# Six stages of a two-layer diffusion trunk in a new order: opening, short convolutions, attention's end, first head, output projections' banks, last token tile

## The chip, the cores and the metric

The kernel runs on one core of one Trainium2 chip. The time is the device time of one execution in microseconds, lower is better; what is compared is the median of several executions of the same program. The core has five engines with queues of their own: TensorE (PE, matrix products into PSUM), VectorE (DVE), ScalarE (ACT), GpSimd (POOL) and SyncE (SP), whose queue issues almost all of this kernel's transfers.

## The reference

Two groups of tokens, 128 prompt tokens and 1024 latent tokens of 1024 features, go through the same two layers in float32. The modulation of each layer (six vectors per group: shift, scale, gate for the mixer and for the feed-forward part) is a product of a condition vector with w_mod.

```python
for l in range(DEPTH):                      # DEPTH = 2
    sh1, sc1, gt1, sh2, sc2, gt2 = split(silu(cond) @ w_mod[l] + b_mod[l], 6)
    h = x * (1 + sc1) + sh1
    if l % 2 == 0:
        q, k, v, bg, cg, xi = split(h @ w_in)       # 8 heads, 2 KV heads, width 64
        att = attend(rope(rms(q)), rope(rms(k)), v) # latent tokens also see 256 cached keys
        o = concat([att, bg * dwconv(cg * xi)]) @ w_out
    else:
        o = hgrn(h)                                 # two directions of a gated recurrence
    x = layer_norm(ALPHA * x + gt1 * o)
    a, g = split(dwconv((x * (1 + sc2) + sh2) @ w_up))
    x = layer_norm(ALPHA * x + gt2 * ((silu(g) * a) @ w_down))
```

dwconv is a convolution over three neighbouring tokens, feature by feature. The outputs are x of both groups, the prompt's keys and values and the recurrence's states.

## The kernel before

**Tiling.** The nine token tiles of 128 (tile 0 the prompt, 1 to 8 the latent tokens) are kept as transposed activations with features on the partitions; a product for one block of 128 output features runs over three chunks of some 386 token columns (c = 0, 1, 2) and eight blocks of the contraction (k). Every product of the large matrices is made of three matmuls on split operands, hi x hi, hi x lo and lo x hi (`mm3`, L92 to L95). A weight block is loaded by `wraw` (L97: 512 KB, two buffers, SP's queue) and split by `wsplit` (L103): the rounded part hi by ACT (L108), the remainder lo by POOL or DVE (L109).

**Opening** (L369 to L516). Per block b of the contraction the first modulation is computed (`modulation`, L415), the activations are modulated and transposed (`modulate`, L444), and the key columns' products of that block are put between (psk, 3 banks). The pool pdS has 5 banks. The value columns (j = 5) follow after the opening in full (`feature`, L516).

**Query, keys, values and short convolutions** (L527 to L671). For each of four groups of 128 features three features are computed (L648 on): the first is copied by ACT, the second multiplied by it (pr, L658) and convolved by ACT and two DVE taps (L661, L662), the third multiplied by the result (sc, L667). Beside them stand seven chunks of later modulation. A chunk (`mod_chunk`, L146) is four loads of 512 KB into two buffers, 16 accumulations on DVE (macc, L170 and L172), eight transposes on TensorE (L181), two reductions (L183) and two additions (L184). `mod_steps` (L190) does the same for the feed-forward layers with loads of 256 KB and eight matmuls against a column of ones (L220).

**Attention** (L673 to L897). Steps of scores, exponentials (ACT), probability tiles PT and value products; PE and ACT issue in written order there (`manual_schedule`, L861). Inside such a region the named engines issue in the order of the program; for all others, and outside, a planner orders the instructions by simulated costs. Every fifth PT is copied by ACT and rounded by POOL (L797 on). Behind the steps a group's finish (L823 to L859) transposes the outputs, scales them and stores them, split, as rows of rhsa. The convolution sums are split into rhsb (L889 to L895: ACT for hi, POOL and DVE in turn for lo).

**Output projection** (`out_projection`, L919). Eight units of weights (two blocks of k and half the columns each); units 0 and 1 are loaded in here, unit n > 2 in a ring of five. The first half of the columns is computed for tiles 8, 7, 6 ahead of the rest. `pt_` (2 banks, transpositions) is opened before `pd` (3 pairs of banks, psd).

**Feed-forward** (`ffn_up`, L1011, and `ffn_down`, L1310). ffn_up has N0 = 6 plain features and then products with combined operands; the first four operands (`operand`, L1110: hi by ACT L1126, lo by POOL) are made behind conv(4). In ffn_down the last token tile is handled like the others: `settle`, L1461 (gate), `ln_sums` (L262), then `ln_affine` (L307).

**Recurrence** (L1527 on). In the first head five jobs of the layer norm are put between chunk steps (list later0, L1889). `recurrence_out` (L2041) has the same two pools as out_projection; jobs in its list todo are taken at t < 2 in addition. `tail1` (L2099) is the last layer norm's affine step.

## Time and profile before

| what | us |
|---|---|
| median of 3 executions | 3229.24 (3228.61 to 3229.68) |
| the profiled execution, its own time | 3231.56 |
| its span, first to last instruction | 3229.8 |
| TensorE busy in it | 3131.4 (97%) |
| DVE, POOL, ACT busy | 2264.6, 1414.8, 1284.4 |
| mean granted clock of TensorE | 0.99 |

TensorE bounds nearly all of the span, so the views to read are those that show where it does not run or runs at the lower clock: its waits by releaser, and the table of stretches, which has the granted clock beside the busy time. Only then are the timelines of the other engines of use, each at one of those places, to see what the engine that released TensorE had done until then. The tail behind the last matmul is read from the timelines of DVE, ACT and POOL.

### The profile page before, as it was taken

To read this page: it belongs to the slowest core of one execution; us is meant where nothing else is said; L and a number is where in the kernel's file an instruction comes from. 1 tells how busy PE (TensorE), PEld (TensorE's weight loads), DVE (VectorE), ACT (ScalarE), POOL (GpSimd) and SP (SyncE) were. 2 spreads that over 40 slices of the span, in tenths; PEclk is the share of its full clock that TensorE was granted. 3 is DMA by queue.
4 is the path that set the end of the run, shared out by engine and by line. 5 is a ranking of instruction groups with operands and counts; after the bars stand their busy time and mean duration, and the time that the engine had idled before them with its cause. 6 is when DMAs were issued, how large, how long until landed. Compare 5 with 4: busy or idle time off the path is not lost. (4 is left out here: it accounts for less than half of the span.)

```text
span 3229.8 us, 48748 instructions
## 1 busy us (share of the span) xinstructions
PE 3131.4 (97%) x19231; PEld 2909.9 (90%) x19231; DVE 2264.6 (70%) x3111; ACT 1284.4 (40%) x2165; POOL 1414.8 (44%) x1014
## 2 busy tenths in 40 slices
PE   7999999899999999999999999999999999999997
PEld 6998788789999998887999999999779999998886
DVE  6777888538988875676566676655656889675356
ACT  4410988333333334215433334333544333335112
POOL 6721233335545443573244343333425554444464
PEclk9999999999999999999999999999999999999999
DMA  7143000322322326542222222211331323225452
GB/s 218 41 132 97 1 1 1 124 85 65 95 89 93 87 97 207 179 160 71 97 83 80 65 68 79 63 51 44 125 118 48 96 84 98 67 78 191 151 172 80
DMA packets 267477, 305.42 MB, mean 95 GB/s; under 512 B 19588, under 2 KB 200016, under 8 KB 267249
## 3 DMA queue, kind: packets, MB, share of 16 engines
q1 hardware_dynamic: 266160, 299.49, 29.2%
q8 instruction: 152, 2.49, 0.3%
q0 software_dynamic: 1088, 2.82, 0.3%
q14 instruction: 77, 0.62, 0.1%
...
## 5 line engine op out<-in xcount | busy, mean ns | idle before, releaser
L1127 POOL TENSOR_TENSOR wlo<-S,whi 128x512 fp32r<-128x512 f32 x152 | 243.1, 1613 | 252.5 <-ACT whi L1126 251.8
L109 POOL TENSOR_TENSOR wlo<-wraw,whi 128x1024 fp32r<-128x1024 f32 x78 | 197.3, 2533 | 206.2 <-ACT whi L108 206.1
L93 PE MATMUL psd<-whi,s 128*128 128x512 f32 x720 | 283.8, 394 | 1.0 <-DVE u L1271 0.9
L95 PE MATMUL psd<-whi,s 128*128 128x512 f32 x720 | 283.8, 394 | 0.0
L94 PE MATMUL psd<-wlo,s 128*128 128x512 f32 x720 | 283.8, 394 | 0.0
L1155 DVE SCALAR_TENSOR_TENSOR t<-u,fcw,t 128x1156 f32<-128x1156 f32 x152 | 264.8, 1760 | 13.8 <-ACT t L1150 11.1
L95 PE MATMUL psq<-T,wlo 128*128 128x290 f32 x912 | 270.7, 297 | 0.0
L94 PE MATMUL psq<-T,whi 128*128 128x290 f32 x912 | 270.2, 296 | 0.0
L93 PE MATMUL psq<-T,whi 128*128 128x290 f32 x912 | 270.0, 296 | 0.0
L1682 POOL TENSOR_TENSOR X<-X,tot 128x384 f32<-128x384 f32 x144 | 169.3, 1176 | 225.3 <-PE pss L1676 212.4
L1127 POOL TENSOR_TENSOR wlo<-wraw,whi 128x512 fp32r<-128x512 f32 x114 | 183.1, 1606 | 171.6 <-ACT whi L1126 153.7
L108 ACT ACTIVATE whi<-wraw 128x1024 fp32r<-128x1024 f32 x130 | 136.8, 1054 | 289.6 <-DMA wraw<-in_ffn_w_down_dram 118.8
L1126 ACT ACTIVATE whi<-S 128x512 fp32r<-128x512 f32 x152 | 92.9, 627 | 321.4 <-DVE S L1105 247.2
L1385 DVE TENSOR_TENSOR y<-y,psd 128x512 f32<-128x512 f32 x144 | 97.9, 684 | 168.0 <-PE psd L95 167.4
L213 DVE SCALAR_TENSOR_TENSOR macc<-mraw,sil,macc 128x512 f32<-128x512 f32 x182 | 189.5, 1080 | 9.0 <-DMA mraw<-in_w_mod_dram 9.0
L93 PE MATMUL psu<-h,whi 128*128 128x388 f32 (+1 forms) x504 | 176.6, 351 | 11.6 <-DVE sc L667 6.5
L94 PE MATMUL psu<-h,whi 128*128 128x388 f32 (+1 forms) x504 | 176.0, 349 | 2.0 <-POOL h L456 2.0
L93 PE MATMUL psp<-s,whi 128*128 128x384 f32 x480 | 174.7, 364 | 0.0
L95 PE MATMUL psu<-h,wlo 128*128 128x388 f32 (+1 forms) x504 | 174.6, 346 | 0.0
L1682 DVE TENSOR_TENSOR X<-X,tot 128x384 f32<-128x384 f32 x144 | 111.6, 775 | 88.0 <-PE pss L1676 85.8
L94 PEld LDWEIGHTS psq<-T,whi 128*128 128x128 f32 x912 | 172.2, 189 | 0.0
L93 PE MATMUL psp<-h,whi 128*128 128x384 f32 x480 | 172.2, 359 | 0.0
...
## 6 DMA issues: line engine op xcount, KB each, us to landing
...
```

Of the source, the lines that this page charges most:

```text
L93: mm(ps, l[0], r[0], start=start, stop=False)
L94: mm(ps, l[0], r[1], start=False, stop=False)
L95: mm(ps, l[1], r[0], start=False, stop=stop)
L108: nc.scalar.activation(hi[:, :n], raw[:, :n], AF.Copy)
L109: (eng or nc.gpsimd).tensor_tensor(lo[:, :n], raw[:, :n], r32(hi[:, :n]), op=ALU.subtract)
L213: nc.vector.scalar_tensor_tensor(acc[:, cond, :], raw, sil[:, cond, k:k + 1], acc[:, cond, :], op0=ALU.mult, op1=ALU.add)
L1126: nc.scalar.activation(hi, src, AF.Copy)
L1127: nc.gpsimd.tensor_tensor(lo, src, r32(hi), op=ALU.subtract)
L1155: nc.vector.scalar_tensor_tensor(t, u[:, :, c0:c0 + HO], taps(p + NF * x)[c0], t, op0=ALU.mult, op1=ALU.add)
L1385: nc.vector.tensor_tensor(y[t][:, cols], y[t][:, cols], ps, op=ALU.add)
L1682: eng.tensor_tensor(x, x, t4[:, :, :, 1 - half].unsqueeze(3).to_broadcast([P, 2, nb, hh]), op=ALU.mult)
```

## The change

Six places are rewritten; what is computed stays the same.

- Opening: the value columns of chunks c = 2 and 1 are accumulated beside the keys in a pool of their own (puV, psv, 2 banks; pdS shrinks from 5 to 3), c = 0 follows after it; their sums are copied by ACT first thing in the next stage.
- Short convolutions: the seven chunks are made by `mod_steps`, whose last step (the matmuls and the addition) is put off by one place (`ends`); the region has a written order for DVE and PE, with 7 to 18 steps per group.
- Attention's end: the last five PT tiles do not go by POOL; the last steps, the first two weight units of the output projection, the finish and the splitting of the convolution sums (DVE alone) are in written order on all engines.
- First head: the place at which the jobs of later0 are taken moves.
- Output projections: the pools pd and pt_ change places; the first products of out_projection run by halves of k; one extra job of recurrence_out is taken at t = 4 instead of t = 0; in ffn_up operand 0 precedes conv(4).
- Last token tile of layer 1: sums, statistics and affine step by halves of the columns, in PSUM.

```diff
...
-    def mod_steps(chunks, pool, bank, bufs=1, steps=1):
+    def mod_steps(chunks, pool, bank, bufs=1, steps=1, ends=None):
...
                 if k == 0:
-                    acc = pool.tile([P, 2, 512], F32, tag="macc", name="macc")
+                    acc = pool.tile([P, 2, 512], F32, tag="macc", bufs=1 if ends is None else 2, name="macc")
...
                 load()
+            def end(l=l, c0=c0, acc=acc):
+                ps = bank()
+                for cond in range(2):
+                    for f in range(4):
+                        mm(ps[:, 4 * cond + f:4 * cond + f + 1], acc[:, cond, f * P:(f + 1) * P], ones, start=True,
+                           stop=True)
+                nc.vector.tensor_tensor(mods[:, l, :, c0:c0 + 4], ps[:, 0:8].rearrange("p (c f) -> p c f", f=4),
+                                        colA[:, l * 48 + c0:l * 48 + c0 + 4].unsqueeze(1).to_broadcast([P, 2, 4]),
+                                        op=ALU.add)
+            if ends is not None:
+                ends.append(end)
+                continue
             yield from [True] * steps
...
+            end()
...
+    qv = ExitStack()
+    pv = qv.enter_context(tc.tile_pool(name="puV", reuse_waits="tile", bufs=1, space=PSUM))
     with ExitStack() as st:
-        pd = st.enter_context(tc.tile_pool(name="pdS", reuse_waits="tile", bufs=5, space=PSUM))
+        pd = st.enter_context(tc.tile_pool(name="pdS", reuse_waits="tile", bufs=3, space=PSUM))
...
         psk = pu.tile([P, 3, 512], F32, tag="u", name="psu")
+        psv = pv.tile([P, 2, 512], F32, tag="v", name="psv")
...
                     b == 0, b == KT - 1)
+            for c in (2, 1):
+                a = 1 + c * OW
+                mm3(psv[:, c - 1, :OW], (wval[0][:, b, :], wval[1][:, b, :]), (hT[0].k(b, a, OW), hT[1].k(b, a, OW)),
+                    b == 0, b == KT - 1)
...
         wkey = wload(wcols(w_in, 512), KT, P)
+        wval = wload(wcols(w_in, 640), KT, P)
...
         st.enter_context(qk)
+        fTv = wk.tile([P, SW], F32, tag="fT", bufs=2, name="fT")
+        nc.scalar.activation(fTv[:, OW:].rearrange("p (a b) -> p a b", b=OW), psv[:, :, :OW], AF.Copy)
+        qv.close()
...
         for j in (4, 5, 0, 1, 2, 3):
-            ps = psk if j == 4 else feature(pus[(j + 1) % 2], j * P, OW, 1)
-            fT = work([P, SW], "fT")
-            nc.scalar.activation(fT.rearrange("p (a b) -> p a b", b=OW), ps[:, :, :OW], AF.Copy)
+            if j == 5:
+                ps, fT = pus[0].tile([P, 3, 512], F32, tag="u", name="psu"), fTv
+                for k in range(KT):
+                    mm3(ps[:, 0, :OW], (wval[0][:, k, :], wval[1][:, k, :]),
+                        (hT[0].k(k, 1, OW), hT[1].k(k, 1, OW)), k == 0, k == KT - 1)
+                nc.scalar.activation(fT[:, :OW], ps[:, 0, :OW], AF.Copy)
+            else:
+                ps = psk if j == 4 else feature(pus[(j + 1) % 2], j * P, OW, 1)
+                fT = work([P, SW], "fT")
+                nc.scalar.activation(fT.rearrange("p (a b) -> p a b", b=OW), ps[:, :, :OW], AF.Copy)
...
+    oun = []
+    def out_unit(n):
+        hf, kk = n // 4, n % 4
+        return (ins["attn_w_out"][0][2 * kk * P:2 * (kk + 1) * P, hf * 512:(hf + 1) * 512]
+                .rearrange("(k p) f -> p k f", p=P), 2, 512)
...
         wk = st.enter_context(tc.tile_pool(name="wkc", reuse_waits="tile", bufs=1))
-        accp, mbufs = wk, 2
...
         pd = st.enter_context(tc.tile_pool(name="pdC0", reuse_waits="tile", bufs=2, space=PSUM))
-        for j in range(4):
+        ends = []
+        mod = mod_steps([mod_todo.pop(0) for _ in range(7)], wk, lambda: pd.tile([P, 512], F32, tag="d", name="mps"), 4,
+                        1, ends)
+        def beside(n):
+            old = list(ends)
+            ends.clear()
+            for _ in range(n):
+                next(mod, None)
+            for f in old:
+                f()
+        st.enter_context(tc.manual_schedule(engines={ET.DVE, ET.PE}))
+        for j, (n0, n1, n2) in enumerate(((1, 3, 3), (6, 6, 6), (6, 6, 6), (7, 7, 0))):
...
             nc.scalar.activation(cg, ps[:, :, :IW], AF.Copy)
-            mod_finish(1)
-            mod_chunk(*mod_todo.pop(0), pd, "d")
+            beside(n0)
...
             nc.vector.scalar_tensor_tensor(yv, pr[:, :, 2:2 + OW], cw[2], yv, op0=ALU.mult, op1=ALU.add)
-            mod_finish(1)
-            if j < 3:
-                mod_chunk(*mod_todo.pop(0), pd, "d")
+            beside(n1)
...
                                     op=ALU.mult)
-        mod_finish()
+            beside(n2)
+        beside(0)
+        assert next(mod, None) is None and not ends
...
             PTs[i] = PT
-            if i % 5 == 5 - 1:
+            if i % 5 == 5 - 1 and i < len(steps) - 5:
...
+        PVL = 4
+        total = len(steps)
+        def step(i):
+            p = i + LEAD
...
+            turn["after"] = piece(*pieces[p]) if 0 <= p < total else None
         with tc.manual_schedule(engines={ET.PE, ET.Activation}):
...
-        for i in sorted(later):
-            for f in later[i]:
-                f()
+            for i in range(-LEAD - 3, total - 1):
+                step(i)
         rhsb = [hp.tile([P, 4, PW], F32R, tag=f"h{q}1", name=f"rb{q}") for q in range(2)]
-        for a, b in ((768, SW), (384, 768), (0, 384)):
+        def second(a, b):
...
                 nc.scalar.activation(hi, sc32[:, j, a:b], AF.Copy)
-                (nc.vector if j % 2 else nc.gpsimd).tensor_tensor(rhsb[1][:, j, a:b], sc32[:, j, a:b], r32(hi),
-                                                                  op=ALU.subtract)
+                nc.vector.tensor_tensor(rhsb[1][:, j, a:b], sc32[:, j, a:b], r32(hi), op=ALU.subtract)
+        with tc.manual_schedule(engines=ALL):
+            raws = [wraw(*out_unit(n)) for n in range(2)]
+            step(total - 1)
+            step(total)
+            oun.append(wsplit(*raws[0], eng=nc.vector))
+            for i in range(total + 1, total + PVL):
+                step(i)
+            oun.append(wsplit(*raws[1], eng=nc.vector))
+            ends = [f for i in sorted(later) for f in later[i]]
+            for f in ends[:2]:
+                f()
+            second(768, SW)
+            for f in ends[2:]:
+                f()
+            for a in (384, 0):
+                second(a, a + 384)
...
         wk = prj.enter_context(tc.tile_pool(name="wk3", reuse_waits="tile", bufs=1))
+        pd = prj.enter_context(tc.tile_pool(name="pdB", reuse_waits="tile", bufs=3, space=PSUM))
         pt_ = prj.enter_context(tc.tile_pool(name="ptB", reuse_waits="tile", bufs=2, space=PSUM))
-        pd = prj.enter_context(tc.tile_pool(name="pdB", reuse_waits="tile", bufs=3, space=PSUM))
...
         def w_unit(n):
-            hf, kk = n // 4, n % 4
-            return wload(w_out[2 * kk * P:2 * (kk + 1) * P, hf * 512:(hf + 1) * 512]
-                         .rearrange("(k p) f -> p k f", p=P), 2, 512, (wk, 5) if n > 2 else None,
-                         nc.vector if n % 2 else None)
+            return wload(*out_unit(n), (wk, 5) if n > 2 else None, nc.vector if n % 2 else None)
...
         rows = wk.tile([P, 2, D], F32, name="rows")
-        units = [w_unit(n) for n in range(2)]
+        units = oun
...
 
-        def products(t, hf):
+        def products(t, hf, ks=range(KT)):
             o = oidx(t)
-            if hf == 0:
+            if t not in pss:
                 pss[t] = pd.tile([P, 2, 512], F32, tag="d", name="psd")
-            for k in range(KT):
+            for k in ks:
...
 
-        for t in (8, 7, 6):
-            products(t, 0)
+        for ks in (range(4), range(4, KT)):
+            for t in (8, 7, 6):
+                products(t, 0, ks)
...
                 nc.sync.dma_start(sd[l][n // 2 - 1], cvs.pop(n - 2))
+            if n == N0 - 1:
+                pr[P0] = (raws.pop(N0 + 1)[0], raws.pop(N0)[0])
+                operand(0)
...
             if n == N0 - 1:
-                pr[P0] = (raws.pop(N0 + 1)[0], raws.pop(N0)[0])
-                for o in range(4):
+                for o in range(1, 4):
...
+            def last_tile():
+                add, st = nc.vector.tensor_tensor, lp.tile([P, 2, 6], F32, tag="bst", name="bst")
+                mv = lp.tile([P, 4], F32, tag="bmw", name="bmw")
+                ps = pw.tile([P, 2, 512], F32, tag="w", name="psw")
+                halves = [slice(hf * 512, (hf + 1) * 512) for hf in range(2)]
+                def sums(hf):
+                    p = ps[:, hf, :]
+                    add(p, p, rows[:, cond_of(0), halves[hf]], op=ALU.mult)
+                    add(p, p, y[0][:, halves[hf]], op=ALU.add)
+                products(ps[:, 0, :], gi, 0, [NU - 4, NU - 3])
+                for f in behind:
+                    f()
+                end[0]()
+                sums(0)
+                end[1]()
+                nc.vector.bn_stats(st[:, 0, :], ps[:, 0, :])
+                products(ps[:, 1, :], gi, 0, [NU - 2, NU - 1])
+                sums(1)
+                nc.vector.bn_stats(st[:, 1, :], ps[:, 1, :])
+                nc.vector.bn_aggr(mv[:, 0:2], st)
+                nc.vector.tensor_scalar(mv[:, 2:3], mv[:, 1:2], EPS, None, op0=ALU.add)
+                x = x1_tile()
+                def one(a, op, cols):
+                    nc.gpsimd.tensor_tensor(x[:, cols], (x if a else y[1])[:, cols], gb[:, a, cols], op=op)
+                one(0, ALU.mult, halves[0])
+                nc.gpsimd.tensor_tensor(mv[:, 3:4], mv[:, 2:3], mhalf[:, 0:1], op=ALU.pow)
+                one(0, ALU.mult, halves[1])
+                for hf, cols in enumerate(halves):
+                    nc.vector.scalar_tensor_tensor(ps[:, hf, :], ps[:, hf, :], mv[:, 0:1], gb[:, 0, cols],
+                                                   op0=ALU.subtract, op1=ALU.mult)
+                for hf, cols in enumerate(halves):
+                    nc.vector.scalar_tensor_tensor(y[0][:, cols], ps[:, hf, :], mv[:, 3:4], gb[:, 1, cols],
+                                                   op0=ALU.mult, op1=ALU.add)
+                    nc.sync.dma_start(outs[0][0][:, cols], y[0][:, cols])
+                for cols in halves:
+                    one(1, ALU.add, cols)
+                    nc.sync.dma_start(outs[1][0, 0:P, cols], x[:, cols])
             for t in range(NT - 1, -1, -1):
+                if l and t == 0:
+                    last_tile()
+                    return y
...
             for n, _ in enumerate(chunk_steps(w0[a], evs[a], c)):
-                if later0 and n % 4 == 1 and (c < 2 or a or n > 4):
+                if later0 and n % 4 == 1 and (c < 2 or 8 * a + n > (4, 12)[len(later0) == 4]):
...
     def recurrence_out():
+        pd = prj.enter_context(tc.tile_pool(name="pdH", reuse_waits="tile", bufs=3, space=PSUM))
         pt_ = prj.enter_context(tc.tile_pool(name="ptH", reuse_waits="tile", bufs=2, space=PSUM))
-        pd = prj.enter_context(tc.tile_pool(name="pdH", reuse_waits="tile", bufs=3, space=PSUM))
...
                     todo.pop(0)(pbank, tmp)
-                if hf and todo and t < 2:
+                if hf and todo and t in (4, 1):
...
         v, g = nc.vector, nc.gpsimd
-        eng = [(slice(0, 512), (v, v)), (slice(512, D), (v, g))] if t == 0 else [(slice(0, D), (v, g))]
-        return [lambda: ln_affine(y[t], gb, x1_tile(), dst, eng)]
+        return [lambda: ln_affine(y[t], gb, x1_tile(), dst, [(slice(0, D), (v, g))])]
...
```

## Rows read from the trace of the kernel before

**Rows 1.** The page's first section: engine, busy us, share of the span, instructions.

```profile
PE 3131.4 (97%) x19231; PEld 2909.9 (90%) x19231; DVE 2264.6 (70%) x3111; ACT 1284.4 (40%) x2165; POOL 1414.8 (44%) x1014
```

**Rows 2.** TensorE's waits, whole span: tile and line, releaser, us, times, longest.

```profile
PE psu L93 <- DVE sc L667: 6.5, 1, 6.5
PE pss L348 <- ACT psw L285: 4.7, 1, 4.7
...
PE psq L93 <- ACT whi L1126: 3.1, 2, 1.6
PE psl L348 <- DVE ht L356: 2.8, 3, 1.6
```

**Rows 3.** Table of stretches: PE, PEld, DVE, ACT, POOL busy, granted clock, DMA, GB/s.

```profile
16.00:56.00 40.00, 33.20 (x191) 24.55 (x192) 27.98 (x43) 22.98 (x38) 22.44 (x20) 0.87 1.10 304
...
224.00:232.00 8.00, 6.02 (x26) 5.70 (x25) 8.00 (x11) 2.21 (x2) 3.17 (x1) 0.79 0.76 194
240.00:256.00 16.00, 9.54 (x42) 9.29 (x41) 12.48 (x19) 2.09 (x2) 2.34 (x1) 0.68 0.65 189
...
576.00:596.00 20.00, 11.54 (x36) 8.07 (x35) 14.67 (x12) 10.40 (x19) 13.07 (x9) 0.66 0.47 157
2408.00:2420.00 12.00, 8.92 (x37) 8.05 (x36) 7.88 (x20) 6.36 (x8) 3.88 (x4) 0.72 0.30 89
```

**Rows 4.** Timeline of TensorE: start, us, line, operation, count; two stretches.

```profile
194.83 0.34 PE L93 MATMUL psu<-h,whi 128*128 128x388 f32 x1
...
196.95 1.04 PE L181 MATMUL mps<-ident,macc 128*128 128x128 f32 x8
...
908.78 1.84 PE L220 MATMUL psq<-ones,macc 128*128 128x1 f32 x16
```

**Rows 5.** Timeline of DVE in the convolutions; in brackets idle before and releaser.

```profile
185.62 3.55 DVE L172 SCALAR_TENSOR_TENSOR macc<-mraw,sil,macc 128x512 f32<-128x512 f32 x2
...
243.01 4.04 DVE L172 SCALAR_TENSOR_TENSOR macc<-mraw,sil,macc 128x512 f32<-128x512 f32 x4 [5.59 <-DMA mraw<-in_w_mod_dram]
246.97 1.35 DVE L667 TENSOR_TENSOR sc<-psu,yv 128x1158 f32<-128x1158 f32 x1
```

**Rows 6.** Groups of DVE's instructions, 143.8 to 318.6 us: busy us, mean ns.

```profile
L172 DVE SCALAR_TENSOR_TENSOR macc<-mraw,sil,macc 128x512 f32<-128x512 f32 x98 | 77.8, 854 | 13.7 <-DMA mraw<-in_w_mod_dram 13.7
L183 DVE TENSOR_REDUCE mods<-mps 128x4 f32<-128x512 f32 x12 | 7.7, 679 | 7.3 <-PE mps L181 7.3
```

**Rows 7.** Timeline of POOL, the same convolution.

```profile
185.32 2.64 POOL L109 TENSOR_TENSOR wlo<-wraw,whi 128x1024 fp32r<-128x1024 f32 x1 [10.32 <-ACT whi L108]
```

**Rows 8.** Timeline of ACT at attention's end.

```profile
575.76 2.60 ACT L893 ACTIVATE rb<-sc 128x390 fp32r<-128x390 f32 x6
...
591.66 1.06 ACT L108 ACTIVATE whi<-wraw 128x1024 fp32r<-128x1024 f32 x1 [2.18 <-DMA wraw<-in_attn_w_out_dram]
...
606.33 1.06 ACT L108 ACTIVATE whi<-wraw 128x1024 fp32r<-128x1024 f32 x1 [5.03 <-DMA wraw<-in_attn_w_out_dram]
```

**Rows 9.** Timeline of DVE at attention's end.

```profile
576.73 3.93 DVE L894 TENSOR_TENSOR rb<-sc,rb 128x390 fp32r<-128x390 f32 x3
...
584.40 3.36 DVE L109 TENSOR_TENSOR wlo<-wraw,whi 128x1024 fp32r<-128x1024 f32 x1
```

**Rows 10.** Timeline of DVE at the first operands of ffn_up, layer 0.

```profile
789.68 4.45 DVE L1071 TENSOR_TENSOR ra<-held,ra 128x580 fp32r<-128x580 f32 x3
```

**Rows 11.** Timeline of DVE at the last token tile.

```profile
3214.72 1.22 DVE L1461 TENSOR_TENSOR psw<-psw,rows 128x1024 f32<-128x1024 f32 x1
...
3221.11 2.78 DVE L311 TENSOR_TENSOR x<-y,gb 128x512 f32<-128x512 f32 x1 [0.23 <-ACT y L293]
```

**Rows 12.** Timeline of POOL at the last token tile.

```profile
3225.36 1.26 POOL L312 TENSOR_TENSOR x<-x,gb 128x512 f32<-128x512 f32 x1 [2.01 <-issue]
```

**Rows 13.** Timeline of ACT, normalization of token tile 1.

```profile
3213.76 1.24 ACT L293 ACTIVATE y<-y,bmv 128x1024 f32<-128x1024 f32 x1 [1.10 <-DVE bmv L292]
```

**Rows 14.** The SP queue's waits, 0 to 340 us: us, times, longest.

```profile
SPq L160 <- DVE macc L172: 93.0, 26, 10.4
```

49 lines of the change are left out of this document (17 added, 32 removed).

## The prediction

> **What bounds the kernel now.** I read the page's first section to see which engine could set the time. TensorE is busy for 3131.4 of 3229.8 us [rows 1]. That leaves 98.4 us of idle time in the whole span, and no edit here removes a matmul. So time can only come from those 98.4 us, from stretches at the lower clock, and from the tail behind the last matmul. The second view is TensorE's waits by releaser: the reader is to see that they are many and small, the largest single one 6.5 us, and which of them belong to lines that the diff touches [rows 2]. The third is the table of stretches, because a wait costs twice here: the granted clock is below 1.00 in and behind each stretch with gaps [rows 3]. At the lower of the two levels (1.2 against 2.4 GHz) a matmul takes twice its time, so a stretch of b busy us at mean granted clock c loses about b x (1 - c). The profiled execution took 3231.56 us, of which 3229.8 are the span; 1.8 us lie around it. It is 2.3 us above the median of 3229.24, so I work out the sum as a difference and take it from either.
>
> **Opening.** The change moves 48 of the 72 matmuls of the value columns (two of three token chunks) between the key products. Twelve products of this width start 2.12 us apart, from 194.83 to 196.95, so one costs 0.177 us [rows 4] and 48 cost 8.5. Between 16 and 56 us TensorE has 40 - 33.20 = 6.8 us idle and loses 33.20 x 0.13 = 4.3 to the clock [rows 3]: room for at most the 8.5. Against that: the loads run at a share of 1.10 and 304 GB/s there [rows 3], full, and the value weights (512 KB) now come in among them, 0.5 MB / 304 GB/s = 1.7 us later for all that is queued on SP behind; three banks instead of five serve the modulation and transposes; the last blocks' products have little idle time to fill; and the new copy of the value sums on ACT must release two banks before the third chunk can start (about 1 us). I take 6 of 8.5 filled, less 1.7, 1 and 1 for these: a gain of 2.5, from -2 (nothing filled, the late load paid) to 5.
>
> **Short convolutions.** TensorE stands still twice here: 8.00 - 6.02 = 2.0 us between 224 and 232 us [rows 3], where the product pr (L658) is late, and 6.5 for the product sc [rows 2]. The windows around them lose 6.02 x (1 - 0.79) = 1.3 and 9.54 x (1 - 0.68) = 3.1 us to the clock [rows 3]. Together 12.9 us. Their cause is DVE's order: sc (L667) at 246.97 sat behind four modulation accumulations that had themselves waited 5.59 us for their load [rows 5]. The written order puts pr, the two taps and sc at fixed places and at most 7 steps of accumulation between, with four smaller loads in flight; I take the 12.9 as gone. It pays for that: eight matmuls against ones per chunk instead of eight transposes. The transposes of a chunk are busy for 1.04 us, and the matmuls against ones, which the feed-forward layers already use, for 1.84 [rows 4]. So 7 x 0.80 = 5.6 us more on TensorE. The reductions go, 12 x 0.68 = 8.2 us of DVE [rows 6], which hides nothing. At the end the last product sc and the last chunk come behind the last feature: pr, two taps and the ACT copy between them, of about sc's size and so 1.35 each [rows 5], and 7 steps of two accumulations are 4 x 1.35 + 14 x 0.85 = 17.3 us [rows 6], against one feature of 72 x 0.177 = 12.7. That is up to 4.6 late; in the kernel before the last chunk's reductions end late here too, so I take 1 us lost net. Sum: 12.9 - 5.6 - 1 = 6.3, taken as 6. Ends: 1 (one of the two waits stays) and 9 (the small matmuls fall into idle time).
>
> Two accumulations took 3.55 us at 185.62, beside the 2.64 us of POOL's weight remainder at 185.32 [rows 5, 7]; their mean over 98 is 0.854 [rows 6]. So one such meeting costs 3.55 - 2 x 0.854 = 1.8 us of DVE, and one ahead of each of the four sc would take 7 us back; the second rival counts half of it. The Trainium skill ("SBUF — State Buffer", section "SBUF: two separate sides") says that a DVE operation with two SBUF inputs and a GpSimd operation that reads SBUF share one pair of ports, which the one that starts first keeps for its whole instruction. By that rule, with which the row agrees, this part and the next, which put more of such work on DVE in a fixed order, can lose.
>
> **Attention's end.** From 576 to 596 us TensorE is busy for 11.54 of 20 us at a clock of 0.66 [rows 3]: 8.5 idle and 3.9 lost to the clock, 12.4 in all. The chain is visible on ACT and DVE: six copies of the convolution sums at 575.76 and three subtractions at 576.73 (3.93 us) stand ahead of the last probability tile, and a weight remainder of 3.36 us at 584.40 ahead of the last attention transposition [rows 8, 9]. Written order moves them behind; the last five tiles also skip POOL. All subtractions now go to DVE, 12 x 1.3 = 15.7 us, of which the later ones lie beside the first products, and the products are split so that k 0 to 3 need attention's heads alone. What is late next is the weights. Unit 2's copy came at 591.66 and unit 6's at 606.33, 14.7 us for two pairs through two buffers [rows 8]. The chain starts when unit 0's remainder releases its buffer, at about 587.8 on DVE's side [rows 9]; now it comes before the last attention steps, about 8 us earlier on one buffer and, with unit 1 behind the last step, 5 on the other. So the whole 12.4 can't be had: I take 8, between 5 and 12.4.
>
> **First head.** The 4.7 us wait of the transposition behind layer norm's sum [rows 2] belongs to the first job that is taken off the list, whose place (step 5) does not move; the four later jobs do, by four steps. 0, from -1 to 4.7.
>
> **ffn_up and the banks.** The 3.1 us for the first split weights [rows 2] go in both layers if operand 0 stands ahead of conv(4). Conv's own DVE work moves back, and with it the three remainders of held sums, 4.45 us at 789.68 [rows 10], for which the products of the third buffer then wait instead. So I take 1, from 0 to the 3.1 plus as much again at the lower clock. In the recurrence's output projection the window 2408 to 2420 has 3.1 us idle and 8.92 x 0.28 = 2.5 lost to the clock [rows 3], and 2.8 us of waits for transposed rows [rows 2]. One job moves forward from t = 0 to t = 4; the next buffer's weights come at their own pace, so I take 2 of the 5.6, from 0 to 5.6. Opening pd before pt_ exchanges banks and adds no instruction.
>
> **Last token tile.** This is tail: all of it counts. Before, the chain from the last product to the last addition is 3214.72 (sums) to 3225.36 + 1.26 = 3226.62 [rows 11, 12]. By halves, the first half's sums are done during the second half's products, squares and ACT's passes go, and DVE has two sums (0.6 each, half of 1.22 [rows 11]), one statistic, four passes of about 0.65. POOL is then the longest: two multiplications and two additions at 1.26 [rows 12] and one power, 5.6 us, from when tile 1 is normalized, at 3213.76 + 1.24 = 3215.00 [rows 13], at the earliest 3220.6. With some 2 us of collisions, as the pass of 2.78 us at 3221.11 shows, where half a row should take about 0.6 [rows 11], the end is at 3222.6: 4 us gained, from 2 to 6.
>
> **Sum.** 2.5 + 6 + 8 + 0 + 1 + 2 + 4 = 23.5 us. 3231.56 - 23.5 = 3208.1 for the profiled execution, 3229.24 - 23.5 = 3205.7 for the median. I predict 3205.7.
>
> **Rivals.** (1) More: all stalls vanish and the clock stays up. 5 + 9 + 11 + 1 + 5 + 4 + 5 = 40 us, 3189. For it: each stretch loses to the clock as much as to waits; against: weights at attention's end and held sums at ffn_up are next. (2) Given back: the weight units don't come earlier, since SP's queue, which the planner still orders, has other loads first, the opening's load is late, and lockouts take from the convolutions. 0 + 2 + 4 + 0 + 0 + 1 + 3 = 10 us, 3219. For it: loads in SP's queue already wait 93.0 us for accumulations up to 320 us [rows 14]. (3) Slower: in the convolutions the SP queue is in order, and a weight load stands behind a modulation load that waits for DVE to free one of four buffers, while DVE, now in written order, waits for TensorE's feature. A weight unit needs about 4 us of load (from 584.40 + 3.36 = 587.8 to 591.66), about 1.1 of copy and 2.64 of remainder [rows 7 to 9], 7.7 in all, against 12.7 of feature. It decides if the load is issued over 5 us after the feature before has started. Issued 10.5 us after it, each of five features is late by 5.5, which costs 27 us: 3229.2 - 17.5 (the other parts) + 27 = 3239. Against it: four buffers hold 1.7 us of DVE work each. (4) Nothing: the planner already gets the same order; 3229. Against it: the new orders are written out.
>
> **Chances.** The forecast with its own range of 3198 to 3214: 0.58. (1) 0.14, (2) 0.18, (3) 0.07, (4) 0.03. The range to 8 in 10 takes the forecast, most of (1) and most of (2): 3188 to 3221. A measurement of this kernel can tell 0.2%, 6.5 us, from no change. Faster by that (below 3222.8): forecast, (1) and most of (2), 0.86. Same: 0.07. Slower (above 3235.7): 0.07.
>
> **What would show it.** Between 140 and 320 us no wait for sc or pr and a clock of 1.00. The first output product follows the last attention tile by some 10 us rather than 14, and waits for a split weight appear in its second half. ffn_up's wait for whi moves to the held remainders. The last addition ends 4 us sooner behind the last matmul. A wait for whi or wlo inside the convolutions would make rival 3 right; key products late before 56 us would make the opening's -2 right.

## The result, and the profile after

The changed kernel takes 3236.53 us (median of 19 runs, 3234.16 to 3239.52), the kernel before 3228.89 in as many runs beside it: a ratio of 1.0024, interval 1.0017 to 1.003. It is 7.6 us slower where 23.5 us less were predicted. Its profiled execution took 3234.8 us, with a span of 3233.0: 3.2 us more than the profile of before. The profile of before lies 2.7 us above its median and that of after 1.7 below, so what the two traces show of the 7.6 is 3.2.

The page's line for TensorE: 56 instructions more, as the change adds them, 4.4 us busier (before: [rows 1]).

```profile
PE 3135.8 (97%) x19287; PEld 2914.0 (90%) x19287; DVE 2239.0 (69%) x3100; ACT 1283.0 (40%) x2163; POOL 1402.3 (43%) x1007
```

TensorE's waits, whole span: tile and line, releaser and its line, us, times, longest.

```profile
PE psw L93 <- DVE bst L1522: 7.8, 1, 7.8
...
PE psu L93 <- ACT cg L695: 6.7, 1, 6.7
PE psu L93 <- DVE y L287: 5.3, 1, 5.3
...
PE pss L353 <- ACT psw L290: 3.2, 1, 3.2
PE psu L93 <- DVE y L1033: 2.7, 1, 2.7
PE psq L94 <- DVE h L1125: 2.4, 3, 1.1
PE psq L94 <- DVE ra L1125: 2.4, 3, 1.1
```

The 6.5 for sc and the 3.1 for whi [rows 2] are gone; the 4.7 of the transposition has become 3.2 (the row of pss L353). Four places have new rows: the last tile (L1522), the convolutions (cg), the feed-forward layers' start (L287, L1033) and their operands (L1125). These six rows hold 27 us.

The table of stretches (columns as in [rows 3]):

```profile
16.00:56.00 40.00, 33.83 (x222) 26.73 (x223) 28.92 (x47) 24.18 (x40) 24.88 (x22) 1.00 1.04 298
160.00:176.00 16.00, 9.27 (x44) 8.94 (x43) 11.82 (x18) 4.42 (x6) 11.98 (x11) 0.84 0.25 74
...
230.00:246.00 16.00, 16.00 (x98) 16.00 (x98) 14.13 (x21) 2.09 (x2) 3.86 (x2) 1.00 0.84 145
575.00:595.00 20.00, 18.10 (x77) 14.36 (x76) 13.58 (x21) 12.27 (x21) 4.10 (x2) 0.91 0.49 164
2408.00:2420.00 12.00, 7.29 (x31) 7.32 (x32) 6.52 (x18) 6.08 (x7) 2.23 (x4) 0.72 0.45 134
3206.00:3222.00 16.00, 8.23 (x26) 6.05 (x25) 7.36 (x13) 4.97 (x6) 7.02 (x5) 0.69 0.24 98
```

Beside [rows 3]: the opening runs at 1.00 instead of 0.87, TensorE no longer stops between 230 and 246 us, and attention's end is busy for 18.10 of 20 us instead of 11.54. What the change meant to do there, it did. The losses are at 160 to 176 us and at 3206 to 3222, where there were none of this size.

Where the time went is best seen from points that both kernels pass. For each the table has the start of the same instruction in both traces, after less before, and what each part gave between them.

| point | before, us | after - before | part | gave | predicted |
|---|---|---|---|---|---|
| first copy of PT in attention | 334.2 | -1.1 | opening and convolutions | -1.1 | -8.5 |
| last layer-norm step of layer 0's mixer | 706.0 | -9.2 | attention's end | -8.1 | -8 |
| products of the held operand (psq from rb) | 799.4 | -4.1 | banks and operand, layer 0 | +5.1 | -0.5 |
| last step of the recurrence | 2283.6 | -3.0 | first head | +1.1 | 0 |
| first product from s, layer 1's ffn_up | 2514.9 | +0.7 | output projection, banks, operand, layer 1 | +3.7 | -2.5 |
| last instruction | 3229.8 | +3.2 | last token tile | +2.5 | -4 |

Attention's end came as predicted, the opening and the convolutions together gave an eighth of their gain, and the other four rows lost time. A row of one trace can be read to about 2 us: the four other kernels below with the same opening and convolutions (banks, last tile, operand, four parts) start attention at 333.30 to 334.83 us, against 333.06 here, so the 1.1 can't be told from nothing.

**The convolutions' first wait.** Timeline of ACT after, two stretches, and TensorE's product behind them (start, us, line, operation, count, idle before and releaser):

```profile
92.23 1.06 ACT L108 ACTIVATE whi<-wraw 128x1024 fp32r<-128x1024 f32 x1 [10.68 <-PE psu L94]
...
94.21 0.48 ACT L626 ACTIVATE qn<-pst 128x384 f32<-128x384 f32 x1
...
171.35 0.31 ACT L661 ACTIVATE qtok<-qn 128x128 f32<-128x128 f32 x1 [4.76 <-DVE qn L636]
171.57 1.12 ACT L695 ACTIVATE cg<-psu 128x1164 f32<-128x1164 f32 x1
```

```profile
172.75 0.69 PE L93 MATMUL psu<-h,whi 128*128 128x386 f32 x1 [6.73 <-ACT cg L695]
```

cg is the first copy in the new stage's memory, which the query stage's tiles still hold: it goes only behind the last query's copy at 171.35. In the kernel before it stood behind the same copy, only 1.5 us sooner (ACT, then TensorE's first product of the third feature):

```profile
169.81 0.31 ACT L638 ACTIVATE qtok<-qn 128x128 f32<-128x128 f32 x1 [5.99 <-DVE qn L613]
170.03 1.12 ACT L653 ACTIVATE cg<-psu 128x1164 f32<-128x1164 f32 x1
```

```profile
171.46 0.34 PE L93 MATMUL psu<-h,whi 128*128 128x386 f32 x1
```

There cg ended at 171.15 and TensorE came at 171.46, 0.3 us later, so it did not wait. After the change it comes at 172.75 - 6.73 = 166.02, 5.4 us sooner, and meets the same chain. Part of the chain's lateness is in the first fence (tested below): at 92.23 ACT splits a weight for which it stood still for 10.68 us, and the third key tile's copy is queued behind it.

**The feed-forward layers' start.** TensorE's first products after, in layers 0 and 1:

```profile
694.29 0.41 PE L93 MATMUL psu<-ra,whi 128*128 128x388 f32 x1 [2.67 <-DVE y L1033]
```

```profile
2412.71 0.66 PE L93 MATMUL psu<-h,whi 128*128 128x388 f32 x1 [5.32 <-DVE y L287]
```

They wait for DVE to finish the last token tile (L1033 and L287 read its sums). With pd opened first, the banks that ffn_up's first sums get are taken to be ones that psd of this tile still holds; putting the order back (below) tests it.

**The operands.** TensorE after, behind ffn_up's sixth feature:

```profile
785.06 0.40 PE L94 MATMUL psq<-ra,whi 128*128 128x290 f32 x1 [0.61 <-DVE ra L1125]
...
786.82 0.40 PE L94 MATMUL psq<-ra,whi 128*128 128x290 f32 x1 [0.69 <-DVE ra L1125]
...
788.57 0.50 PE L94 MATMUL psq<-ra,whi 128*128 128x290 f32 x1 [1.09 <-DVE ra L1125]
```

DVE after:

```profile
783.85 4.67 DVE L1125 TENSOR_TENSOR ra<-held,ra 128x580 fp32r<-128x580 f32 x3
```

The wait for whi is gone. In its place the products wait three times for the remainders that DVE makes of the held sums (L1125), behind conv's taps as before. These start 5.8 us sooner than at 789.68 [rows 10], but TensorE reaches their products 7.8 us sooner, at 784.08 instead of 791.90; before, it waited for one of them, 0.79 us. Layer 1 has the same at 2504 to 2509.

**The last token tile.** TensorE, DVE and POOL after:

```profile
3208.82 0.40 PE L95 MATMUL psw<-whi,s 128*128 128x512 f32 x1
3216.99 0.79 PE L93 MATMUL psw<-whi,s 128*128 128x512 f32 x1 [7.77 <-DVE bst L1522]
3217.58 0.63 PE L94 MATMUL psw<-wlo,s 128*128 128x512 f32 x1
...
3221.84 0.63 PE L95 MATMUL psw<-whi,s 128*128 128x512 f32 x1
```

```profile
3213.44 0.69 DVE L1514 TENSOR_TENSOR psw<-psw,rows 128x512 f32<-128x512 f32 x1
...
3216.16 0.16 DVE L297 TENSOR_TENSOR bmv<-bmv 128x1 f32<-128x1 f32 x1 [1.31 <-POOL bmv L294]
3216.24 0.69 DVE L1522 BATCH_NORM_STATS2 bst<-psw 128x6 f32<-128x512 f32 x1
```

```profile
3213.28 2.34 POOL L317 TENSOR_TENSOR x<-x,gb 128x1024 f32<-128x1024 f32 x1 [1.40 <-issue]
3215.58 0.55 POOL L294 TENSOR_TENSOR bmv<-bmv,mhalf 128x1 f32<-128x1 f32 x1
```

The first half's products end at 3209.22. The second half's, into the other bank of the same tile, start only when DVE has read the first half's statistics, 7.77 us later, and then run 0.43 us apart instead of 0.23. DVE is that late because tile 1's normalization is ahead of it, with a power on POOL (L294) that is queued behind a 2.34 us addition. DVE was behind TensorE in the kernel before too: its sums of this tile started at 3214.72 [rows 11], the last product at 3210.95:

```profile
3210.95 0.40 PE L95 MATMUL psw<-whi,s 128*128 128x512 f32 x1
```

### The profile page after: what moved, and what is told of

Read it like the earlier page. It is cut to its first block, busy times and chain, and to the rows that moved or that the text cites. A ratio compares the mean times of both kernels' runs of the same rounds, so it can differ in the third digit from the quotient of the medians.

```text
span 3233.0 us, 48921 instructions
## 1 busy us (share of the span) xinstructions
PE 3135.8 (97%) x19287; PEld 2914.0 (90%) x19287; DVE 2239.0 (69%) x3100; ACT 1283.0 (40%) x2163; POOL 1402.3 (43%) x1007
## 5 line engine op out<-in xcount | busy, mean ns | idle before, releaser
L213 DVE SCALAR_TENSOR_TENSOR macc<-mraw,sil,macc 128x512 f32<-128x512 f32 x280 | 265.8, 998 | 17.4 <-DMA mraw<-in_w_mod_dram 17.4
L93 PE MATMUL psu<-h,whi 128*128 128x388 f32 (+1 forms) x488 | 170.5, 349 | 15.2 <-ACT cg L695 6.7
L95 PEld LDWEIGHTS psq<-T,wlo 128*128 128x128 f32 x912 | 172.2, 189 | 0.3 <-POOL wlo L1181 0.3
L93 PEld LDWEIGHTS psq<-T,whi 128*128 128x128 f32 x912 | 172.3, 189 | 0.0
L94 PEld LDWEIGHTS psq<-T,whi 128*128 128x128 f32 x912 | 172.3, 189 | 0.0
```

Of the source, the lines that this page charges most:

```text
L93: mm(ps, l[0], r[0], start=start, stop=False)
L94: mm(ps, l[0], r[1], start=False, stop=False)
L95: mm(ps, l[1], r[0], start=False, stop=stop)
L213: nc.vector.scalar_tensor_tensor(acc[:, cond, :], raw, sil[:, cond, k:k + 1], acc[:, cond, :], op0=ALU.mult, op1=ALU.add)
```

## The experiments

**Undoing one part of the changed kernel.** Four kernels, each the changed one with one part taken back or mended.

Banks: the pools in the old order, in both projections.

```diff
-        pd = prj.enter_context(tc.tile_pool(name="pdB", reuse_waits="tile", bufs=3, space=PSUM))
         pt_ = prj.enter_context(tc.tile_pool(name="ptB", reuse_waits="tile", bufs=2, space=PSUM))
+        pd = prj.enter_context(tc.tile_pool(name="pdB", reuse_waits="tile", bufs=3, space=PSUM))
```

> The changed kernel with pt_ opened ahead of pd again in both output projections, all else as changed. Theory: the exchange put the first feed-forward sums on banks that the last token tile's psd still holds; the two new waits of TensorE (2.67 us at 694.29 for y L1033, 5.32 us at 2412.71 for y L287) go, and the 0.69 us at the start of the recurrence's projection come back. In the ledger against the kernel before, the changed kernel lost 2.9 us between 706 and 725 and 3.1 us between 2339 and 2435, so about 5 us less than the changed kernel: 3231.5. Rival: the weights or the transposed rows are as late as the banks, so the waits change their name only: within 1.5 us of the changed kernel.

Measured: 3232.11 us, 1.0009 of before [1.0, 1.0019], 4.4 us under the changed kernel's median. The waits behind L1033 and L287 are gone, as the theory had it; at layer 1 one of 2.9 us for a transposed row (releaser ht, L358; 0.8 in the kernel before) stands in their place. The order in which two pools are opened cost between 4 and 5 us.

Last tile: each half of the columns in a tile of its own.

```diff
-                ps = pw.tile([P, 2, 512], F32, tag="w", name="psw")
+                ps = [pw.tile([P, 2, 512], F32, tag="w", name="psw")[:, 0, :] for _ in range(2)]
...
-                    p = ps[:, hf, :]
+                    p = ps[hf]
```

> The changed kernel with the last token tile's two halves in two PSUM tiles in place of two halves of one. Theory: TensorE's 7.77 us wait at 3216.99 for the statistics of the first half is a dependence between the halves of one tile, not of the data; with two tiles the second half's products follow the first half's at 3209 at the full clock and end at about 3212 in place of 3222.5. Then DVE's and POOL's chain for tile 1 is last (its second normalization value at 3216.2), and the end moves from 3229.4 to about 3224: 5.5 us less than the changed kernel, 3231. Rival: the second half's products wait for something else of DVE (the buffer of tile 2, the order of issue), and the time stays within 1.5 us.

Measured: 3232.23 us, 1.0004 [0.9995, 1.0013], 4.3 us less than the changed kernel by the medians, 6.5 by the ratios. TensorE's timeline at the border of the halves and at the end, and DVE's first sum:

```profile
3215.31 0.39 PE L95 MATMUL psw<-whi,s 128*128 128x512 f32 x1
3215.55 0.39 PE L93 MATMUL psw<-whi,s 128*128 128x512 f32 x1
...
3218.10 0.40 PE L95 MATMUL psw<-whi,s 128*128 128x512 f32 x1
```

```profile
3219.92 0.69 DVE L1514 TENSOR_TENSOR psw<-psw,rows 128x512 f32<-128x512 f32 x1
```

There is no wait left and no slower product behind it. So the wait came from the halves sharing one tile; DVE's lateness alone, which is unchanged here, does not make TensorE wait. It does keep the first half's sums from lying beside the second half's products: they start when the last product is done.

Operand 0 behind conv(4) again, with the other three:

```diff
-                operand(0)
             if n:
                 conv(n - 1)
             if n == N0 - 1:
-                for o in range(1, 4):
+                for o in range(4):
```

> The changed kernel with all four first operands of ffn_up behind conv(4) again. Theory: the early operand 0 lets TensorE start some 2 us sooner, and it then waits three times for the remainders of held sums that DVE makes late (2.4 us in each layer, and a clock of 0.88); the ledger lost 2.2 and 1.8 us there, so about 4 us less than the changed kernel: 3232.5. Rival: those losses come from the earlier start of the whole stage and not from this edit; then the waits for the first split weights (1.5 us in each layer) come back and nothing is gained: 0 to 2 us more.

Measured: 3233.15 us, 1.001 [1.0001, 1.0019], 3.4 us less than the changed kernel by the medians, 4.5 by the ratios. The old waits are back, 1.56 and 0.86 at 779.80 and 781.20 us, and cost less than the ones that the new order brought.

The old opening (value columns behind it, five banks):

```diff
-            for c in (2, 1):
-                a = 1 + c * OW
-                mm3(psv[:, c - 1, :OW], ...
...
-        wval = wload(wcols(w_in, 640), KT, P)
```

> The changed kernel with the opening as before (all value products behind it, five banks). Theory: the opening put TensorE some 6 us ahead, but the third feature of the convolutions waits for the copy cg on ACT, which stands behind the last query tile's chain on DVE and POOL; this floor takes the gain back as the 6.73 us wait at 172.75. Without the opening's part the wait shrinks to under 1.5 us and the start of attention moves by less than 2 us: 3235 to 3238.5. Rival: the wait belongs to the written order of the convolutions alone and stays at 5 us or more; then the opening's 5 to 6 us are lost in full: 3242.

Measured: 3230.15 us, 1.0003 [0.9994, 1.0012], 6.8 us faster than the changed kernel by the ratios. Both expectations are wrong: with the rest of the change in place the new opening costs time. In this kernel there is no wait for cg, and attention starts 7.4 us sooner than before.

**One part alone, put into the kernel before.**

Attention's end (the last five PT without POOL, the written order, the first products by halves of k, pools in the old order):

```diff
-            if i % 5 == 5 - 1:
+            if i % 5 == 5 - 1 and i < len(steps) - 5:
...
+        with tc.manual_schedule(engines=ALL):
+            raws = [wraw(*out_unit(n)) for n in range(2)]
+            step(total - 1)
...
```

> The kernel before with attention's end alone changed (last five tiles not by POOL, written order of the last steps, first two weight units early, remainders on DVE, products by halves of k; pools in the old order). Theory: the 8.3 us that the changed kernel gained between the last tile (0.9 us ahead) and the first normalization (9.2 ahead) belong to this stage and are kept: 3229 - 8 = 3221, from 3219 to 3223. Rival: part of them is an effect of the earlier stages' order or is given back at the first feed-forward sums: 3225 or more.

Measured: 3223.92 us, 0.998 [0.9972, 0.9989], 6.5 less, between the two expectations; in the trace 7.0 us from attention's start (333.73, before 334.18) to the last layer-norm step (698.47, before 705.96).

Convolutions:

```diff
+        mod = mod_steps([mod_todo.pop(0) for _ in range(7)], wk, lambda: pd.tile([P, 512], F32, tag="d", name="mps"), 4,
+                        1, ends)
...
+        st.enter_context(tc.manual_schedule(engines={ET.DVE, ET.PE}))
```

> The kernel before with the short convolutions alone changed (modulation by matmuls against ones, written order on DVE and TensorE). Theory: in the changed kernel with the old opening this stage took TensorE from 2.3 to 7.4 us ahead, so 5 us are gained: 3224, from 3222 to 3226, with no wait for pr, sc or cg above 1.5 us and 5.6 us more of small matmuls. Rival: the copy cg is late here too, since ACT is not in the written order: a wait of 3 us or more and 3228 to 3231.

Measured: 3222.68 us, 0.998 [0.9971, 0.9989], 6.5 less. Neither sc nor pr nor cg is waited for, and the clock from 165 to 312 us is 1.00 (before 0.95).

Opening:

```diff
-        pd = st.enter_context(tc.tile_pool(name="pdS", reuse_waits="tile", bufs=5, space=PSUM))
+        pd = st.enter_context(tc.tile_pool(name="pdS", reuse_waits="tile", bufs=3, space=PSUM))
...
+            for c in (2, 1):
+                a = 1 + c * OW
+                mm3(psv[:, c - 1, :OW], ...
```

> The kernel before with the opening's part alone. Theory: it loses by itself, by the late loads and by the weight split that holds ACT's queue ahead of the third key tile; the planner, which orders the convolutions here, can't hide it, since cg stands behind the query chain: 3 to 6 us more, 3232 to 3235. Rival: the loss needs the written order of the convolutions, which fixes TensorE's third feature behind cg; alone the opening gains 1 to 3 us.

Measured: 3223.6 us, 0.9985 [0.9976, 0.9994], 4.8 less. TensorE's waits of this kernel between 62 and 330 us:

```profile
PE psu L93 <- ACT cg L671: 6.7, 1, 6.7
...
PE psu L93 <- DVE pr L676: 1.6, 1, 1.6
...
PE psu L93 <- DVE sc L685: 1.0, 1, 1.0
```

Both expectations are wrong. The wait for cg is there in full and takes more than the lead: the third feature starts at 173.57 us, 2.1 later than before. The gain comes behind it, at the second group's sc (DVE):

```profile
237.96 1.35 DVE L685 TENSOR_TENSOR sc<-psu,yv 128x1158 f32<-128x1158 f32 x1
247.99 4.73 DVE L172 SCALAR_TENSOR_TENSOR macc<-mraw,sil,macc 128x512 f32<-128x512 f32 x7 [8.68 <-DMA mraw<-in_w_mod_dram]
```

The accumulations that wait for a load now stand behind sc, where in [rows 5] they stood ahead of it, and the wait for sc fell from 6.5 to 1.0. The edit does not touch this order; it came out so in the planned order of DVE. So this gain is one that the convolutions' written order takes too, and the two don't add.

Two halves of the opening, to see its costs: three banks instead of five, and the value weights loaded early.

```diff
-        pd = st.enter_context(tc.tile_pool(name="pdS", reuse_waits="tile", bufs=5, space=PSUM))
+        pd = st.enter_context(tc.tile_pool(name="pdS", reuse_waits="tile", bufs=3, space=PSUM))
```

> The kernel before with three banks in place of five in the opening's pool, nothing else changed. It tells the banks from the rest of the opening's part, which as a whole cost 6.8 us by the kernel without it. Theory: the modulation's and transposes' products are paced by the loads, at a share of 1.1 of the queues, and three banks are enough: within 1 us of the kernel before. Rival: they cost 2 us or more, as the end of the modulation's products, 1.3 to 4.1 us later in all kernels with the new opening, would have it.

```diff
         wkey = wload(wcols(w_in, 512), KT, P)
+        wval = wload(wcols(w_in, 640), KT, P)
```

> The kernel before with the value weights loaded and split in the opening, behind the key weights, and used where they were; no value product is moved. Theory: 512 KB at some 310 GB/s put all later loads of the opening 1.7 us back, and the split weights hold one of three buffers through the opening: the modulation's products end 1.5 to 3 us later, and the time is 1.5 to 4 us longer, 3231 to 3233. Rival: the loads have slack, and the delay of the new opening comes from its products: within 1 us.

Measured: 3231.08 us, 1.0009 [1.0, 1.0018], by the ratio 2.9 us more, the rival's size, but with an interval that reaches to none and a trace 0.9 us shorter than that of before, so not settled; and 3228.0, 0.9999 [0.9991, 1.0008], against the theory. In the second trace the modulation ended 5.7 us late, the first pr was 3.2 us late (183.7 instead of 180.5), the last one was on time (305.5 and 305.7): in the convolutions, which wait in the old order, the delay was taken up. A delay ahead of a stage that waits need not be a cost.

**Parts together.** The changed kernel with the four taken back or mended, and the kernel before with three parts (convolutions, attention's end, last tile in two tiles):

```diff
-        psv = pv.tile([P, 2, 512], F32, tag="v", name="psv")
...
-                operand(0)
...
+                ps = [pw.tile([P, 2, 512], F32, tag="w", name="psw")[:, 0, :] for _ in range(2)]
...
```

> The changed kernel with four edits taken out or mended: the old opening, pt_ ahead of pd, all first operands behind conv(4), and the last tile's halves in two PSUM tiles. Theory: the four losses are in places of their own and add up. Against the kernel before, the single kernels stood at -4.8, -6.5, -4.5 and -6.8 us from the changed kernel's +7.7: together -22.6, so 3214, from 3211 to 3217. Rival: they overlap (an earlier start of the feed-forward stage only meets the next wait): 3219 to 3223.

> The kernel before with three parts only: the short convolutions, attention's end, and the last token tile by halves in two PSUM tiles. It is the kernel with four edits back (e7) without the first head's and the recurrence job's new places. Theory: in e7 the first head went from 12.0 to 10.0 us ahead and the recurrence's projection lost another 1.4, so both edits cost time: 3 us less than e7, 3214, with the first head's stage within 0.7 us of neutral. Rival: those losses are noise of one profile or come with any earlier start: within 1 us of e7, 3216 to 3218.

Measured: 3216.98 us, 0.9961 [0.9949, 0.9974], and 3215.82, 0.9961 [0.9948, 0.9973]. By the medians the first lies 19.6 us under the changed kernel, where the four single kernels gave 4.4, 4.3, 3.4 and 6.4, together 18.5: the four losses add up, and with them taken out the rest of the change gains 12.6. The two differ by the places of the layer-norm jobs alone (first head, extra job), which so cost or gain nothing that can be told, as the rival of the second said. In the second one's trace the last tile gave 3.1 us.

The new opening on top of these three:

```diff
+            for c in (2, 1):
+                a = 1 + c * OW
+                mm3(psv[:, c - 1, :OW], ...
...
```

> The three good parts (convolutions, attention's end, mended last tile: 3215.8) and the new opening, with cg's memory as changed. Theory: opening and written convolutions each gain alone (4.6 and 6.5 us) but not together, since one stall takes both gains: the time is 4 to 7 us longer than with the three parts, 3220 to 3223. Rival: what the changed kernel lost came from its other parts, and the gains add: 3211 or 3212.

Measured: 3223.0 us, 0.9978 [0.9969, 0.9987]: by the ratios 5.5 us lost (7.2 by the medians) by a part that gains 4.8 alone. The wait for cg is 6.7.

**Taking the wait for cg away.** First from ACT's side: the third query feature's weight split goes behind the third key tile's copy.

```diff
+                with tc.issue_after(kq) if j == 2 else ExitStack():
+                    ps = psk if j == 4 else feature(pus[(j + 1) % 2], j * P, OW, 1)
...
+                act = nc.scalar.activation(qn, pt[:, :384], AF.Copy)
+                if j == 4:
+                    kq = act.ins
```

> The changed kernel, new opening kept, with one thing moved on ACT: the split of the third query feature's weights is queued behind the copy of the third key tile. Theory: the opening's loss comes from that split, which stood ahead of the key chain and held ACT's queue for 10.7 us (92.23) until TensorE released its buffer; behind it the key chain is 3.6 us later and with it the copy cg. Without it the third key tile is copied at 90.5 in place of 94.2, the wait of 6.73 us for cg falls to about 3, and the time falls by 3 to 4 us: 3233. Rival: the opening's loss comes from its own loads and its three banks; then the wait for cg stays above 5.5 us and the time within 1.5 us of the changed kernel.

Measured: 3234.11 us, 1.0012 [1.0003, 1.0021], 3.9 less than the changed kernel by the ratios, 2.4 by the medians. The copy that started at 94.21 now starts at 90.67. ACT, then TensorE's third feature:

```profile
90.67 0.49 ACT L627 ACTIVATE qn<-pst 128x384 f32<-128x384 f32 x1 [7.14 <-POOL t L651]
...
171.44 1.12 ACT L698 ACTIVATE cg<-psu 128x1164 f32<-128x1164 f32 x1
```

```profile
172.61 0.69 PE L93 MATMUL psu<-h,whi 128*128 128x386 f32 x1 [2.70 <-ACT cg L698]
```

The wait for cg fell from 6.7 to 2.7 us, though cg starts at nearly the same time of its trace. In this trace the opening ends 2.8 us later: the first product behind it (psu from fT, released by ACT) starts at 76.55 us instead of 73.75. Counted from there cg comes 94.9 us behind, where in the changed kernel it was 97.8, as in the kernels above with this opening and this wait (97.80 to 97.85). So the split held the chain back by some 3 us of the 6.7, and the rest of its length stays open.

Then from the memory's side: cg in a pool of its own.

```diff
+    cgp = cgx.enter_context(tc.tile_pool(name="cgp", reuse_waits="tile", bufs=1, side="right"))
...
-            cg = wk.tile([P, 3, IW], F32, tag="cg", bufs=2, name="cg")
+            cg = cgp.tile([P, 3, IW], F32, tag="cg", name="cg")
...
-            yv = wk.tile([P, 3, OW], F32, tag="cg", bufs=2, name="yv")
+            yv = wk.tile([P, 3, OW], F32, tag="yv", name="yv")
```

In the changed kernel:

> The changed kernel with one thing changed: the copy cg of the convolutions' first feature gets memory that the query stage doesn't use (same size, other place). Theory: cg could not be written before the query chain had read its last tiles, since its bytes were theirs; TensorE's third feature waited for it 6.73 us and lost some 2.3 more to the clock. With memory of its own it is copied right behind its feature, at about 155 in place of 171.6, and the time falls by 7 to 9 us, to 3228 or 3229. Rival: the product pr, on DVE behind the same query chain, is the next wait: the wait moves to pr, is 5 us or more, and under 3 us are gained.

In the four parts, without and with the split moved as well:

> As e14, with cg in memory of its own. Theory: without that stall both gains are there: 7 to 9 us less than e14, 2 to 4 less than the three parts, 3212 to 3214. Rival: the split of weights that stands ahead of the key chain and the late loads hold the query chain, and pr or the first attention scores wait for it: no better than the three parts, 3216 or more.

> As e15, with the third query feature's weight split queued on ACT behind the third key tile too. Theory: with cg free, the query chain ends before anything in the convolutions needs it, so an earlier chain is worth nothing: within 1.5 us of e15. Rival: the chain is still the floor (by pr on DVE): 2 us or more less than e15.

Measured: 3232.25 us, 1.0011 [1.0002, 1.002]; 3218.62, 0.9966 [0.9953, 0.9978]; 3217.95, 0.9965 [0.9952, 0.9977]. cg is copied at 159.02 to 161.01 us, the wait is gone in all three, and half of the gain that the theories expected (7 to 9 us) is missing in all three: by the ratios 4.2, 3.9 and 4.2. The next wait is not pr, as the first rival had it, but the last modulation chunk's. In the first of them (TensorE, then DVE, then POOL):

```profile
308.81 1.41 PE L220 MATMUL mps<-ones,macc 128*128 128x1 f32 x6 [4.17 <-DVE macc L213]
```

```profile
295.76 13.56 DVE L213 SCALAR_TENSOR_TENSOR macc<-mraw,sil,macc 128x512 f32<-128x512 f32 x14
```

```profile
296.01 0.98 POOL L745 TENSOR_SCALAR qr<-qtok 128x512 fp32r<-128x512 f32 x1 [31.51 <-DVE yv L705]
...
297.97 1.72 POOL L750 TENSOR_TENSOR qs<-qs,qr 128x512 f32<-128x512 f32 x1
```

In the changed kernel the same 14 accumulations took 9.36 us, and POOL's preparation of attention's first queries started behind them:

```profile
304.46 9.36 DVE L213 SCALAR_TENSOR_TENSOR macc<-mraw,sil,macc 128x512 f32<-128x512 f32 x14
```

```profile
313.90 0.62 POOL L742 TENSOR_SCALAR qr<-qtok 128x512 fp32r<-128x512 f32 x1 [40.69 <-DVE mods L222]
```

There it was released by the last chunk's addition (L222), in the new layout by a convolution tap (L705), 18 us sooner, and POOL works beside DVE. No run here shows which tile's memory it waits for; only the layout was changed. Each accumulation takes 0.97 us instead of 0.67, each of POOL's short passes 0.98 instead of 0.62. The Trainium skill ("SBUF — State Buffer", section "SBUF: two separate sides") says that DVE operations with two SBUF inputs and GpSimd operations that read SBUF exclude each other on a shared pair of ports; the trace agrees.

That reading was tested by holding POOL back until the 14 are done:

```diff
+            if j == 3:
+                nc.vector.memset(hold[:, 0:1], 1.0)
+                held = nc.gpsimd.tensor_tensor(hold[:, 1:2], hold[:, 0:1], ones, op=ALU.pow)
...
+            with tc.issue_after(held.ins) if not rss else ExitStack():
+                prep(t, i)
```

In the four parts, and in the changed kernel:

> The four parts with cg in memory of its own, and POOL's first query preparation held back until DVE has made the 14 accumulations behind the last pr (a marker that DVE writes and POOL reads; one extra instruction on each). In the version without the hold POOL started this preparation at 297.8 us and the 14 accumulations beside it took 13.55 us, against 9.36 in the kernels where POOL starts at 309 to 314; TensorE then waited 4.2 us for them. Theory (the meeting with POOL, set free by the new memory layout, is what ate the gain): the 14 take 9.4 us again, no wait of L220, and the time falls by some 4 us from 3218.6 to 3213 to 3216, no worse than the three parts without the opening (3215.8). Rival (the opening has nothing left to give once the convolutions are in order, whatever POOL does): the wait goes, another takes its place (the query's transposition ppq behind POOL), and the time stays at 3217 to 3220.

> The same two edits (cg in memory of its own, POOL held) in the changed kernel. Theory: 3232.25 minus 4, so 3227 to 3229.5; with it the pair of edits gives the changed kernel back the 8 to 9 us that the wait for cg and its clock cost. Rival: 3231 to 3233, as without the hold.

Measured: 3215.4 us, 0.9953 [0.994, 0.9965], and 3229.82, 1.0003 [0.9994, 1.0012] (a third of a microsecond outside what was expected; 6.7 under the changed kernel). DVE and POOL in the first:

```profile
296.74 9.36 DVE L213 SCALAR_TENSOR_TENSOR macc<-mraw,sil,macc 128x512 f32<-128x512 f32 x14
```

```profile
306.28 0.55 POOL L710 TENSOR_TENSOR hold<-hold,ones 128x1 f32<-128x1 f32 x1 [40.82 <-DVE hold L709]
```

The 14 take 9.36 us again, the wait of L220 is gone, and only 2.5 us for the first query's transposition (behind POOL) is left (1.3 in the kernel before, there behind the modulation). In the second kernel attention starts 9.4 us sooner than before, where the changed kernel had 1.1. Four parts with these two mends are the fastest version found: by the ratios 15 us faster than before, where the same four without the mends gain 7. Against the three parts without the opening its interval overlaps, so what the opening adds once all is mended is not settled; the traces give it 0.7 us at attention's start, less than the 1.2 by which the last two kernels differ there with the same stages.

## Why the prediction was wrong

**The parts that were read from stalls.** Alone, the convolutions gave 6.5 us (predicted 6) and attention's end 6.5 (8); the last tile, mended, gave 3.1 in its trace (4). These stretches were read rightly, and the terms are of the right size. The opening gave 4.8 alone (2.5), but that is luck: its lead was lost at cg, and the gain came from another order at sc, which the prediction did not have. The clock came back with the gaps, as the sum supposed: 0.87 to 1.00 in the opening, 0.66 to 0.91 at attention's end. Between 140 and 320 us nothing waits for sc or pr, as forecast. The sign "last addition ends 4 us sooner behind the last matmul" is met in appearance only: from the last matmul's start to the end of the span it was 18.9 us and is 11.2, because that matmul comes 10.9 us later; with two tiles it is 15.5.

**The sum.** The first step that failed is adding "2.5 + 6", with the opening's gain taken as kept to the end. What is late next behind the opening was not asked: the keys and queries on ACT and DVE, with a memory that the next stage needs. In the kernel before this chain was done 0.3 us ahead of TensorE, so a lead that the chain did not share had to become a wait; the chain came 1.5 us later instead. The wait cost 6.73 us and, at a clock of 0.84, 9.27 x 0.16 = 1.5 more in the stretch from 160 to 176; the rest of its 16 us belongs to the wait. Together the two parts gave 1.1 where 8.5 were predicted. With cg in memory of its own and POOL held back they gave 9.4.

**"Opening pd before pt_ exchanges banks and adds no instruction."** True, and the wrong question. It decides which banks the next stage's first sums get, and so on whom they wait: 2.67 and 5.32 us. No instruction is added; two waits are. With the pools put back both are gone and 4.4 us return.

**ffn_up.** The step named the cost, the three remainders of held sums for which the products then wait, and took a gain of 1 with a range from 0 up. The bound below nothing was missing. TensorE came 2 us nearer to the remainders and waited for each of the three, in both layers, and the products behind the last wait ran at the lower clock (0.24 us apart instead of 0.13). Measured: a loss of 3.4 to 4.5 us.

**Last token tile.** "The first half's sums are done during the second half's products" failed twice. The second half waits for the first half's readers; no row that the step read has two banks of one tile written and read in turn, and it took the overlap as given without a bound for its absence. And DVE comes too late for the overlap even with two tiles, as it did in [rows 11], 3.8 us behind the last product's start. The first failure costs the 7.77 us of the wait and, at the lower clock, 12 products x 0.2 = 2.4 us: together the 10.2 by which the last matmul comes later than at the stage's start. In two tiles the term is 3.1 of 4.

**The recurrence's projection and the first head.** The window 2408 to 2420 is no better than before (7.29 busy at 0.72): what the earlier job could have given can't be seen beside the bank wait. Neither move showed an effect of its own.

**The rivals.** None was the mechanism. No whi or wlo is waited for in the convolutions, so the third, which alone led to the slower side, was wrong, although the time came out near its 3239. The second had a true part, collisions of DVE and POOL, but they were seen to cost TensorE time only in kernels without the wait for cg. The chance of 0.07 for slower left out the case that several edits at once, each costed near nothing, bring a wait each.

What stays open: 3 of the 7.6 us that separate the medians are in the traces; the rest is the place of each profile among its runs. The new waits were each taken away, and by the medians the kernel got back 4.4 us of the 8.0 that the two bank waits held (one of 2.9 came in their place), 3.4 of some 4 for the operand, 4.3 of the 10.2 at the last tile (the tail behind it is longer then), and 4.3 of the 8.2 at cg, 6.7 with POOL held back. Beyond the 3 us or so of the weight split, what sets the end of the query chain, and so the floor for the opening's lead, was not found.
